# A streaming-encoder trunk on one core: depthwise convolution taps moved from TensorE to ScalarE and GpSimd, three chunks in flight

## The chip, the cores and the metric

The kernel runs on one core of a Trainium2 chip. The metric is device time in microseconds, the median of several executions. A core has TensorE (PE, matrix products into PSUM), VectorE (DVE), ScalarE (ACT), GpSimd (POOL) and SyncE (SP, which here issues the weight loads). PSUM has eight banks; a tile of 128 x 512 float32 fills one.

## The reference

Two layers over 256 tokens of width 2048, in float32. Layer 0 mixes tokens by a Conformer convolution module, layer 1 by latent attention; each is followed by a squared-ReLU MLP. The change touches the convolution module alone:

```python
u = h @ w_pw1 + b_pw1
a, gate = jnp.split(u, 2, axis=-1)
u = a * jax.nn.sigmoid(gate)
u = causal_depthwise_conv(u, w_dw) + b_dw      # 31 taps for each channel
u = jax.nn.silu(layer_norm(u, ln_g, ln_b))
return u @ w_pw2 + b_pw2
```

For each channel the depthwise convolution is a sum of 31 products: the gated row, shifted by w tokens, times one weight for each channel.

## The kernel before, in words

Products of float32 matrices are done as three products of float32r parts: each weight block is split into hi (ScalarE, L154) and lo = raw - hi (L155, on GpSimd in most of the convolution stage).

The 2048 channels are 16 chunks of 128, one channel to a partition, with 256 tokens along the row. The main loop runs c = 1 .. 16; iteration c multiplies chunk c on TensorE (`conv_mm`, L485 to L487, 96 matrix instructions) while the other engines work on chunk c-1. In the order in which they are written, which each engine's queue keeps (the schedule is manual), an iteration holds: weight loads; `glu(c-1)`, where ScalarE takes the sigmoid (L502) and VectorE the gate product (L503) into `ub`, whose 30 leading columns GpSimd clears; the first part of `conv_mm`; weight splits; `pe_taps(c-1)`, which takes the first few taps on TensorE as products with diagonal matrices (L518; ScalarE makes the diagonals, L509) into a PSUM tile `sum`, to which ScalarE adds the bias (L521); `dve_taps`, the remaining taps on VectorE (L552), one SCALAR_TENSOR_TENSOR for each: sum = ub[shifted] * tap + sum; more splits and the rest of `conv_mm`; `to_tokens(c-3)`, which transposes a finished chunk (L579); and GpSimd's addition of the second bias to the residual (L692). Each sum has a tile `sum` of its own, of which it uses half.

Three taps of chunks 1 to 13 go to TensorE, none of chunk 0, six of chunk 14 and 19 of chunk 15. `dve_taps(c)` takes taps of chunk c and of the one before in turn, after four taps of the older chunk alone, and leaves 16 taps of the newest for the next iteration. `ln_stats` puts BATCH_NORM_STATS2 of finished pairs (L589) and a copy of them (L591) between the taps. After the loop come the last transposes, some transposes that keep TensorE busy (`keep_warm`, L220), the LayerNorm (L704, L715, L730 to L737) and the second projection, for which weights are loaded ahead.

The pools of PSUM in this stage are: four tiles `acc` (products, two for each chunk), two `tr` (transposes) and two `sum`.

Of the kernel before, what the change touches and what calls it, by code (L numbers as in the profile page):

```python
# [10 lines left out]
F32 = mybir.dt.float32  # L11
# [3 lines left out]
AF = mybir.ActivationFunctionType  # L15
# [25 lines left out]
PAD_O = 56  # L41
WB = 6
LOOK = WB // 2 - 1
PE_TAPS = (3, 3, 3, 3)
PE_MORE = (3, 16)
LEAD = 4
REST = (16, 12)
N_WARM = 14
N_WARM_LN = (8, 26, 14)
EPS = 1e-6  # L50
# [22 lines left out]
def trunk_kernel(  # L73
# [54 lines left out]
    def nm(s):  # L128
        uid[0] += 1
        return f"{s}_{uid[0]}"  # L130


    def acc_tile():
        return psum["acc"].tile([P, NB], F32, tag="acc", name=nm("acc"))
# [298 lines left out]
    with ExitStack() as cx:  # L433
# [23 lines left out]
        def conv_load(n):  # L457
            if n < NU:
                c, k = n // UC, n % UC * 8
                raws[n] = load(  # L460
                    [rows(conv_w_pw1[0], k, 8, c * P, P), rows(conv_w_pw1[0], k, 8, D + c * P, P)], 8
                )
            elif n < NU + KC // 2:
                raws[n] = load([rows(conv_w_pw2[0], 2 * (n - NU), 2, 0, 2 * NB)], 2)

        def conv_half(n, h):
            if n < NU + KC // 2:
                wjs[n, h] = split_half(raws[n], h, nc.gpsimd if 0 < n + h and n < NU + 2 else nc.vector)
# [10 lines left out]
        def conv_mm(c, k0, nk=4):  # L479
            for k in range(k0, k0 + nk):  # L480
                wh, wl = conv_w(UC * c + k // 8, k % 8)
                for b in range(2):
                    bs = slice(b * P, (b + 1) * P)
                    o = pss[c][b][:, :S]
                    nc.tensor.matmul(o, wh[:, bs], xh(k), start=k == 0, stop=False)  # L485
                    nc.tensor.matmul(o, wh[:, bs], xl(k), start=False, stop=False)  # L486
                    nc.tensor.matmul(o, wl[:, bs], xh(k), start=False, stop=k == KC - 1)  # L487

        pss, ubs, pcs, cas, cts = {}, {}, {}, {}, {}
        n_pe = lambda c: 0 if c == 0 else PE_TAPS[c % 4] + {KC - 2: PE_MORE[0], KC - 1: PE_MORE[1]}.get(c, 0)  # L490
        rest = lambda c: {KC - 2: REST[1], KC - 1: 0}.get(c, REST[0])
        tap = lambda c, w: w_dw[:, w * KC + c : w * KC + c + 1]

        def sum_tile():
            return psum["sum"].tile([P, NB], F32, tag="sum", name=nm("sum"))

        def glu(c):
            ub = ubs[c] = cv2.tile([P, PAD + S], F32, tag="ub", name=nm("ub"), bufs=3)
            nc.gpsimd.memset(ub[:, 0:PAD], 0.0)
            sg = cv2.tile([P, S], F32, tag="sg", name=nm("sg"))  # L500
            va, ga = pss.pop(c)
            nc.scalar.activation(sg, ga[:, :S], AF.Sigmoid, bias=b_pw1[:, KC + c : KC + c + 1])  # L502
            nc.vector.scalar_tensor_tensor(  # L503
                out=ub[:, PAD:], in0=va[:, :S], scalar=b_pw1[:, c : c + 1], in1=sg, op0=ALU.add, op1=ALU.mult
            )

        def diag(c, w):
            dg = cv2.tile([P, P], F32, tag="dg", name=nm("dg"), bufs=16)
            nc.scalar.activation(dg, ident, AF.Copy, scale=tap(c, w))  # L509
            return dg  # L510

        def pe_taps(c, dgs):

            pc = pcs[c] = sum_tile()[:, :S]
            for w in range(n_pe(c)):
                if w == len(dgs):
                    dgs.append(diag(c, w))
                nc.tensor.matmul(pc, dgs[w], ubs[c][:, w : w + S], start=w == 0, stop=w == n_pe(c) - 1)  # L518
            left[c] = list(range(n_pe(c), W))
            if 0 < c < KC - 1:  # L520
                nc.scalar.activation(pc, pc, AF.Identity, bias=b_dw[:, c : c + 1])  # L521
            elif c:

                pcs[c], last_sum[:] = acc_tile()[:, :S], [pc]

        left, last_sum = {}, []

        def ca_part(c):
            if c // 2 not in cas:
                cas[c // 2] = cv2.tile([P, 2, S], F32, tag="ca", name=nm("ca"))  # L530
            return cas[c // 2][:, c % 2, :]

        def dve_tap(c):
            w = left[c].pop(0)
            out = pcs[c]
            if c in (0, KC - 1) and w == n_pe(c):
                nc.vector.tensor_scalar(
                    out, ubs[c][:, w : w + S], scalar1=tap(c, w), scalar2=b_dw[:, c : c + 1],
                    op0=ALU.mult, op1=ALU.add,
                )  # L540
                return
            if c == KC - 1:
                if not left[c]:
                    half = cv2.tile([P, S], F32, tag="half", name=nm("half"), bufs=1)
                    nc.vector.scalar_tensor_tensor(
                        out=half, in0=ubs[c][:, w : w + S], scalar=tap(c, w), in1=out, op0=ALU.mult, op1=ALU.add
                    )
                    nc.vector.tensor_tensor(ca_part(c), last_sum[0], half, op=ALU.add)
                    return
            elif not left[c]:  # L550
                out = ca_part(c)
            nc.vector.scalar_tensor_tensor(  # L552
                out=out, in0=ubs[c][:, w : w + S], scalar=tap(c, w), in1=pcs[c], op0=ALU.mult, op1=ALU.add
            )

        def dve_taps(c, rest, fill):


            n = 0
            while len(left[c]) > rest or left.get(c - 1):  # L560
                if left.get(c - 1):
                    dve_tap(c - 1)
                if n < LEAD and c < KC - 1 and left.get(c - 1):
                    if fill:
                        fill.pop(0)()
                elif len(left[c]) > rest:
                    dve_tap(c)
                n += 1
            while fill:
                fill.pop(0)()  # L570

        def to_tokens(c):

            if c % 2 == 0:
                cts[c // 2] = tr_tile()
            ct = cts[c // 2]
            for t in range(T):
                q = 2 * t + c % 2
                nc.tensor.transpose(  # L579
                    ct[:, q * P : (q + 1) * P], cas[c // 2][:, c % 2, t * P : (t + 1) * P], ident  # L580
                )

        def ln_stats(c):
# [22 lines left out]
        with tc.manual_schedule():  # L606
# [52 lines left out]
                turn(w_dw[:, i * NW : (i + 1) * NW], w_rows[i])  # L659
            conv_split(2)  # L660
            conv_mm(0, 12)
            dgs = []
            fills = []
            for c in range(1, KC + 1):
                n = UC * c
                conv_load(n + 3)
                glu(c - 1)
                fills += ln_stats(c - 4) if c > 3 else []
                fill, fills = fills[: 1 + c % 2], fills[1 + c % 2 :]
                if c < KC:  # L670
                    pss[c] = [acc_tile() for _ in range(2)]
                    conv_mm(c, 0, 2)
                conv_half(n + 1, 0)
                pe_taps(c - 1, dgs)
                conv_half(n + 1, 1)
                dve_taps(c - 1, rest(c - 1), fill)
                conv_load(n + 4)
                if c < KC:
                    conv_mm(c, 2, 6)
                    conv_half(n + 2, 0)  # L680
                    conv_half(n + 2, 1)
                    conv_mm(c, 8)
                    dgs = [diag(c, w) for w in range(min(n_pe(c), 16))]
                if c > 2:
                    to_tokens(c - 3)
                if c < KC:
                    conv_mm(c, 12)
                if 2 <= c < 2 + T * NNB:

                    t, i = divmod(c - 2, NNB)  # L690
                    sl = slice(i * NB, (i + 1) * NB)
                    nc.gpsimd.tensor_tensor(xs[:, t, sl], xs[:, t, sl], b2[:, sl], op=ALU.add)  # L692
            warm(AF.Sqrt)
            keep_warm(ident, N_WARM_LN[0])
            to_tokens(KC - 2)
# [51 lines left out]
            for m in range(NP):  # L747
                if m + 3 < NP:
                    ln_norm(m + 3)
                if m + 2 < NP:  # L750
                    ln_swish(m + 2)
                for j in range(2):
                    k = 2 * m + j
                    wh, wl = conv_w(NU + m, j)
                    for b in range(2):
                        bs = slice(b * NB, (b + 1) * NB)
                        for t in range(T):
                            mm3(ps2[b][t], sh_kt(k, t), sl_kt(k, t), wh[:, bs], wl[:, bs], k == 0, k == KC - 1)
                conv_split(NU + m + 2)
                conv_load(NU + m + 5)  # L760

        ssq, add, prepare = residual_stage(True, g_mlp[0])
        for b in range(2):
# [590 lines left out]
```

## Time and profile before

| what | us |
|---|---|
| median of 3 runs (lowest, highest) | 2014.32 (2014.25, 2014.42) |
| the profiled execution | 2014.3 |
| its span | 2012.4 |
| busy in the span: TensorE | 1989.3 (99%) |
| VectorE | 1217.5 (61%) |
| ScalarE | 966.0 (48%) |
| GpSimd | 209.3 (10%) |
| the chunk loop, first to last gate product (L503) | 31.64 to 222.35 |
| last chunk summed (L548, start and duration) | 232.39, 0.42 |

The profile is of one execution, whose own time lies 1.9 us above its span. A line of the timeline gives the start, the length of a run of like instructions, the engine, the source line, the operation, the tile written and those read, and how many; in brackets stands how long the engine had been idle and who ended that. Instructions of one engine overlap: the start of the next, not the end of this one, tells what one costs. `PE` matrix instructions of float32 come as two records for each product.

### The profile page before, as it was taken

The numbers are of one execution on the slowest core, as the hardware profiler recorded it, in microseconds if no ns is written. First come the engines' busy times: TensorE is split into PE (matmuls) and PEld (weight loads), VectorE is DVE, ScalarE is ACT, GpSimd is POOL, SyncE is SP. The second block draws the span as 40 slices with busy tenths as digits, with TensorE's granted clock in tenths as the row PEclk, the third lists the DMA queues.
The fourth block names the chain that finished last, engine by engine and source line by source line (L and its number), as shares of the span: only waits on it lengthen the run. The fifth ranks groups of instructions, "written<-read, shape, count | busy, mean of one in ns | idle before, by whom it ended". The sixth has DMA issues, their size and how long they took to land.

```text
span 2012.4 us, 28002 instructions
## 1 busy us (share of the span) xinstructions
PE 1989.3 (99%) x11144; PEld 1743.9 (87%) x11144; DVE 1217.5 (61%) x1806; ACT 966.0 (48%) x1372; POOL 209.3 (10%) x156
## 2 busy tenths in 40 slices
PE   7999999999999999999999999999999999999998
PEld 7999888888888888888889998888888888888886
DVE  6999866665554466555546675665654545565453
ACT  5444665544434354444446665544543334454443
POOL 5887300000000000000000510000000000000000
PEclk9999999999999999999999999999999999999999
DMA  7555355666555666555545445666655556665553
GB/s 237 168 168 168 126 188 179 198 189 188 189 197 199 189 189 188 189 192 192 192 144 186 131 146 171 206 190 188 189 192 198 197 188 188 189 189 194 199 192 105
DMA packets 243266, 367.58 MB, mean 183 GB/s; under 512 B 15416, under 2 KB 89792, under 8 KB 242880
## 3 DMA queue, kind: packets, MB, share of 16 engines
q1 hardware_dynamic: 242400, 364.68, 56.9%
q8 instruction: 87, 1.43, 0.3%
q10 hardware_dynamic: 736, 1.12, 0.2%
q14 instruction: 43, 0.35, 0.0%
HBM read 363.68 MB, written 2.10 MB: 182 GB/s over the span
## 4 chain that ended last, share of the span: by engine, by line
PE 96%; DVE 2%; ACT 1%; DMA 0%; issue 0%; POOL 0%; SPq 0%; ACTq 0%; DVEq 0%
PE acc L399 23%; PE acc L182 16%; PE acc L180 16%; PE acc L181 16%; PE acc L400 12%; PE acc L486 3%; PE acc L485 3%; PE acc L487 3%; PE sum L518 1%; PE tr L237 1%; DMA xs<-in_x 0%; PE acc L1128 0%; PE acc L992 0%; PE acc L994 0%; PE acc L993 0%
## 5 line engine op out<-in xcount | busy, mean ns | idle before, releaser
L155 DVE TENSOR_TENSOR lo<-raw,hi 128x1024 fp32r<-128x1024 f32 (+2 forms) x629 | 759.7, 1211 | 694.8 <-ACT hi L154 682.9
L154 ACT ACTIVATE hi<-raw 128x1024 fp32r<-128x1024 f32 (+1 forms) x696 | 723.6, 1046 | 787.3 <-PE acc L181 451.2
L399 PE MATMUL acc<-xt,hi 128*128 128x512 f32 x2048 | 710.6, 390 | 0.0
L400 PE MATMUL acc<-xt,lo 128*128 128x256 f32 x2048 | 577.7, 282 | 0.0
L399 PEld LDWEIGHTS acc<-xt,hi 128*128 128x128 f32 x2048 | 384.4, 188 | 80.5
L180 PE MATMUL acc<-hi,gh 128*128 128x512 f32 x1024 | 398.6, 389 | 0.0
L182 PE MATMUL acc<-lo,gh 128*128 128x512 f32 x1024 | 398.4, 389 | 0.0
L181 PE MATMUL acc<-hi,gl 128*128 128x512 f32 x1024 | 398.4, 389 | 0.0
L400 PEld LDWEIGHTS acc<-xt,lo 128*128 128x128 f32 x2048 | 387.1, 189 | 0.1
L182 PEld LDWEIGHTS acc<-lo,gh 128*128 128x128 f32 x1024 | 192.2, 188 | 39.9
L180 PEld LDWEIGHTS acc<-hi,gh 128*128 128x128 f32 x1024 | 192.2, 188 | 39.8
L181 PEld LDWEIGHTS acc<-hi,gl 128*128 128x128 f32 x1024 | 192.2, 188 | 39.7
L552 DVE SCALAR_TENSOR_TENSOR sum<-ub,w_dw,sum 128x256 f32<-128x256 f32 x404 | 168.5, 483 | 2.8 <-ACT sum L521 0.7
L155 POOL TENSOR_TENSOR lo<-raw,hi 128x1024 fp32r<-128x1024 f32 x67 | 159.3, 2400 | 56.6 <-ACT hi L154 56.6
L485 PE MATMUL acc<-xt,hi 128*128 128x256 f32 x512 | 147.0, 287 | 0.0
L486 PE MATMUL acc<-xt,hi 128*128 128x256 f32 x512 | 143.2, 280 | 1.0 <-DVE xt L193 1.0
L487 PE MATMUL acc<-xt,lo 128*128 128x256 f32 x512 | 143.0, 279 | 0.0
L486 PEld LDWEIGHTS acc<-xt,hi 128*128 128x128 f32 x512 | 96.3, 188 | 1.6 <-DVE xt L193 1.2
L485 PEld LDWEIGHTS acc<-xt,hi 128*128 128x128 f32 x512 | 96.3, 188 | 0.4
L487 PEld LDWEIGHTS acc<-xt,lo 128*128 128x128 f32 x512 | 96.2, 188 | 0.0
L923 POOL MEMSET pad_kv<- 128x8 f32 x1 | 0.1, 105 | 772.6 <-PE acc L182 772.6
L407 ACT ACTIVATE v<-acc 128x256 f32<-128x256 f32 x128 | 46.3, 381 | 25.4 <-PE acc L400 25.4
(230 smaller groups left out, 1787.1 us busy)
## 6 DMA issues: line engine op xcount, KB each, us to landing
raw<-in_mlp_w SPq DMA_DIRECT2D x256, 1024.0 KB, 5.1
raw<-in_conv_w_pw SPq DMA_DIRECT2D x64, 512.0 KB, 5.1
raw<-in_conv_w_pw SPq DMA_DIRECT2D x16, 1024.0 KB, 4.9
raw<-in_mla_w_o SPq DMA_DIRECT2D x16, 1024.0 KB, 5.2
raw<-in_mla_w_kv_up SPq DMA_DIRECT2D x8, 1024.0 KB, 5.4
raw<-in_mla_w_in SPq DMA_DIRECT2D x8, 576.0 KB, 3.7
raw<-in_mla_w_in SPq DMA_DIRECT2D x4, 1024.0 KB, 6.5
raw<-in_mla_w_q_up SPq DMA_DIRECT2D x16, 256.0 KB, 3.6
```

What stands on the lines that cost most here:

```text
L154: nc.scalar.activation(hi, raw[:, js, :], AF.Copy)
L155: eng.tensor_tensor(lo, raw[:, js, :], hi.bitcast(F32), op=ALU.subtract)
L180: nc.tensor.matmul(ps, sh, mh, start=start, stop=False)
L181: nc.tensor.matmul(ps, sl, mh, start=False, stop=False)
L182: nc.tensor.matmul(ps, sh, ml, start=False, stop=stop)
L399: nc.tensor.matmul(ps[b], wh[:, bs], xhl(k), start=k == 0, stop=False)
L400: nc.tensor.matmul(ps[b][:, :S], wl[:, bs], xh(k), start=False, stop=k == KC - 1)
L407: nc.scalar.activation(v[:, b, :], o[:, S:], AF.Copy)
L485: nc.tensor.matmul(o, wh[:, bs], xh(k), start=k == 0, stop=False)
L486: nc.tensor.matmul(o, wh[:, bs], xl(k), start=False, stop=False)
L487: nc.tensor.matmul(o, wl[:, bs], xh(k), start=False, stop=k == KC - 1)
L552: nc.vector.scalar_tensor_tensor(out=out, in0=ubs[c][:, w : w + S], scalar=tap(c, w), in1=pcs[c], op0=ALU.mult, op1=ALU.add)
```

## The change

- The gate product of all chunks but the last goes to GpSimd: ScalarE first copies the value half with its bias from PSUM to SBUF (`vb`), and GpSimd multiplies it by the sigmoid.
- Tap 0 of those chunks is made on ScalarE, together with the bias, and starts the sum in PSUM. Taps 1 and 2 are made by ScalarE as products in SBUF (`product`), which GpSimd adds (`side_sum`); VectorE adds the result to the sum as one of its steps (the entry `None` in `left`, the 15th of 29).
- Only the last chunk has diagonal products: 22 taps, and four more at the side, which leaves VectorE five taps.
- The sums of two neighbouring chunks share one PSUM tile (`pair_part`), two halves of one bank. In the last pair, chunk 14's sum and the product sum of chunk 15 share it; the VectorE part of chunk 15 has an `acc` tile.
- `dve_taps` keeps up to three chunks in flight: it stops when 20 steps are left in all (16 and 18 in the first two iterations), takes in turn from the two oldest chunks, and lets the newest begin after seven steps.
- The first eight blocks of a chunk's product are written in one piece; splits and side sums move in the order; the addition of the second bias on GpSimd moves from the loop to the second projection.

The core of the diff:

```diff
-PE_TAPS = (3, 3, 3, 3)
-PE_MORE = (3, 16)
-LEAD = 4
-REST = (16, 12)
+LAST_PE = 22
+SIDE = 2
+LAST_SIDE = 4
+JOIN = 14
+LEAD = 7
+REST = (16, 18, 20)
...
+        def pair_part(tiles, c, new):
+
+            if c // 2 not in tiles:
+                tiles[c // 2] = new()
+            return tiles[c // 2][:, c % 2 * S : (c % 2 + 1) * S]
...
+                vb = cv2.tile([P, S], F32, tag="vb", name=nm("vb"))
+                nc.scalar.activation(vb, va[:, :S], AF.Identity, bias=b_pw1[:, c : c + 1])
+                nc.gpsimd.tensor_tensor(ub[:, PAD:], vb, sg, op=ALU.mult)
+
+        def product(c, w):
+            pr = cv2.tile([P, S], F32, tag="tp", name=nm("tp"), bufs=LAST_SIDE + SIDE)
+            nc.scalar.activation(pr, ubs[c][:, w : w + S], AF.Copy, scale=tap(c, w))
+            return pr
...
+        def start_sum(c):
+            w = 0
+            if c < KC - 1:
+                pcs_c = pcs[c] = pair_part(sums, c, sum_tile)
+                nc.scalar.activation(
+                    pcs_c, ubs[c][:, 0:S], AF.Identity, bias=b_dw[:, c : c + 1], scale=tap(c, 0)
+                )
+                w = 1
+            else:
+                pcs[c] = acc_tile()[:, :S]
+                o = pair_part(sums, c, sum_tile)
+                last_sum.append(o)
+                for w in range(LAST_PE):
+                    nc.tensor.matmul(o, dgs[w], ubs[c][:, w : w + S], start=w == 0, stop=w == LAST_PE - 1)
+                w = LAST_PE
+            n = LAST_SIDE if c == KC - 1 else SIDE
+            sides[c] = [product(c, w + i) for i in range(n)]
+            left[c] = list(range(w + n, W))
+            left[c].insert(min(JOIN, len(left[c]) - 1), None)
...
+        def side_sum(c):
+            ps = sides[c]
+            step = 1
+            while step < len(ps):
+                for i in range(0, len(ps) - step, 2 * step):
+                    nc.gpsimd.tensor_tensor(ps[i], ps[i], ps[i + step], op=ALU.add)
+                step *= 2
...
+        def dve_taps(c, fill):
+
+
+            n, last = 0, None
+            lead = 0 if c in (0, KC - 1) else LEAD
+            while sum(len(v) for v in left.values()) > rest(c):
+                ready = [k for k in sorted(left) if left[k] and (k < c or n >= lead)]
+                if not ready:
+                    break
+                k = next((k for k in ready[:2] if k != last), None)
+                if fill and (k is None or n % 2 == 1):
+                    fill.pop(0)()
+                    last = None if k is None else last
+                if k is None:
+                    k = ready[0]
+                dve_tap(k)
+                last = k
                 n += 1
...
                 if c < KC:
                     pss[c] = [acc_tile() for _ in range(2)]
-                    conv_mm(c, 0, 2)
-                conv_half(n + 1, 0)
-                pe_taps(c - 1, dgs)
+                    conv_half(n + 1, 0)
+                start_sum(c - 1)
+                if c == KC:
+                    side_sum(c - 1)
+                    conv_half(n + 1, 0)
                 conv_half(n + 1, 1)
-                dve_taps(c - 1, rest(c - 1), fill)
+                dve_taps(c - 1, fill)
                 conv_load(n + 4)
                 if c < KC:
-                    conv_mm(c, 2, 6)
+                    side_sum(c - 1)
+                    conv_mm(c, 0, 8)
```

More of the change, by code (lines that the diff above doesn't have):

```diff
@@ L487, in conv_mm @@
                     nc.tensor.matmul(o, wl[:, bs], xh(k), start=False, stop=k == KC - 1)
-        pss, ubs, pcs, cas, cts = {}, {}, {}, {}, {}
-        n_pe = lambda c: 0 if c == 0 else PE_TAPS[c % 4] + {KC - 2: PE_MORE[0], KC - 1: PE_MORE[1]}.get(c, 0)
-        rest = lambda c: {KC - 2: REST[1], KC - 1: 0}.get(c, REST[0])
+        pss, ubs, pcs, cas, cts, sides, left = {}, {}, {}, {}, {}, {}, {}
+        rest = lambda c: 0 if c == KC - 1 else REST[min(c, 2)]
         tap = lambda c, w: w_dw[:, w * KC + c : w * KC + c + 1]
@@ L495, in sum_tile, with ca_part @@
             return psum["sum"].tile([P, NB], F32, tag="sum", name=nm("sum"))
+        def pair_part(tiles, c, new):
+            if c // 2 not in tiles:
+                tiles[c // 2] = new()
+            return tiles[c // 2][:, c % 2 * S : (c % 2 + 1) * S]
+        def ca_part(c):
+            return pair_part(cas, c, lambda: cv2.tile([P, 2 * S], F32, tag="ca", name=nm("ca")))
         def glu(c):
@@ L502, in glu @@
             nc.scalar.activation(sg, ga[:, :S], AF.Sigmoid, bias=b_pw1[:, KC + c : KC + c + 1])
-            nc.vector.scalar_tensor_tensor(
-                out=ub[:, PAD:], in0=va[:, :S], scalar=b_pw1[:, c : c + 1], in1=sg, op0=ALU.add, op1=ALU.mult
-            )
+            if c == KC - 1:
+                nc.vector.scalar_tensor_tensor(
+                    out=ub[:, PAD:], in0=va[:, :S], scalar=b_pw1[:, c : c + 1], in1=sg, op0=ALU.add, op1=ALU.mult
+                )
[3 more added lines that the diff above has]
+                nc.gpsimd.tensor_tensor(ub[:, PAD:], vb, sg, op=ALU.mult)
@@ L507, in diag @@
+        def product(c, w):
+            pr = cv2.tile([P, S], F32, tag="tp", name=nm("tp"), bufs=LAST_SIDE + SIDE)
+            nc.scalar.activation(pr, ubs[c][:, w : w + S], AF.Copy, scale=tap(c, w))
+            return pr
         def diag(c, w):
-            dg = cv2.tile([P, P], F32, tag="dg", name=nm("dg"), bufs=16)
+            dg = cv2.tile([P, P], F32, tag="dg", name=nm("dg"), bufs=LAST_PE)
             nc.scalar.activation(dg, ident, AF.Copy, scale=tap(c, w))
             return dg
[L512 to L531, printed above, removed]
+        dgs, last_sum = [], []
+        def start_sum(c):
[4 more added lines that the diff above has]
+                    pcs_c, ubs[c][:, 0:S], AF.Identity, bias=b_dw[:, c : c + 1], scale=tap(c, 0)
+                )
+                w = 1
+            else:
+                pcs[c] = acc_tile()[:, :S]
[8 more added lines that the diff above has]
+            left[c].insert(min(JOIN, len(left[c]) - 1), None)
@@ L533, in dve_tap @@
+        sums = {}
+        def side_sum(c):
[5 more added lines that the diff above has]
+                step *= 2
         def dve_tap(c):
@@ L535, in dve_tap @@
             out = pcs[c]
-            if c in (0, KC - 1) and w == n_pe(c):
+            if w is None:
+                nc.vector.tensor_tensor(out, out, sides[c][0], op=ALU.add)
+                return
+            if c == KC - 1 and w == LAST_PE + LAST_SIDE:
                 nc.vector.tensor_scalar(
@@ L541, in dve_tap @@
                 return
-            if c == KC - 1:
-                if not left[c]:
+            if not left[c]:
+                if c == KC - 1:
                     half = cv2.tile([P, S], F32, tag="half", name=nm("half"), bufs=1)
@@ L549, in dve_tap @@
                     return
-            elif not left[c]:
                 out = ca_part(c)
@@ L554, in dve_tap @@
             )
[L556 to L567, printed above, removed]
+        def dve_taps(c, fill):
[13 more added lines that the diff above has]
+                last = k
                 n += 1
@@ L579, in to_tokens @@
                 nc.tensor.transpose(
-                    ct[:, q * P : (q + 1) * P], cas[c // 2][:, c % 2, t * P : (t + 1) * P], ident
+                    ct[:, q * P : (q + 1) * P], ca_part(c)[:, t * P : (t + 1) * P], ident
                 )
@@ L661, in trunk_kernel @@
             conv_mm(0, 12)
-            dgs = []
             fills = []
@@ L682, in trunk_kernel @@
                     conv_mm(c, 8)
-                    dgs = [diag(c, w) for w in range(min(n_pe(c), 16))]
+                    if c > KC - 4:
+                        dgs.extend(diag(KC - 1, w) for w in range(len(dgs), min(len(dgs) + 8, LAST_PE)))
                 if c > 2:
@@ L687, in trunk_kernel @@
                     conv_mm(c, 12)
[L688 to L692, printed above, removed]
             warm(AF.Sqrt)
@@ L760, in trunk_kernel @@
                 conv_load(NU + m + 5)
+                t, i = divmod(m, NNB)
+                sl = slice(i * NB, (i + 1) * NB)
+                nc.gpsimd.tensor_tensor(xs[:, t, sl], xs[:, t, sl], b2[:, sl], op=ALU.add)
         ssq, add, prepare = residual_stage(True, g_mlp[0])
```

## The prediction

> **What bounds the kernel now.** I read the busy table first, then the table by stretches of the conv stage, then the chain of work that ended last, then the timelines of VectorE, ScalarE and TensorE. The whole kernel is TensorE at 99%. For the loop over chunks (43 to 222 us):
>
> ```profile
> 43.00:222.00 179.00, 178.80 (x1454) 176.22 (x1453) 169.07 (x419) 85.25 (x147) 144.04 (x78) 1.00 0.56 166
> ```
>
> The columns are TensorE, its weight loads, VectorE, ScalarE, GpSimd: TensorE has no gap, but VectorE is busy for 169.1 of 179 us, so it can give back 10 us at most. What the diagonal products take stands in the chain:
>
> ```profile
> 68.94 1.31 PE sum L518 x6
> 81.68 1.31 PE sum L518 x6
> ...
> 209.16 2.61 PE sum L518 x12
> ```
>
> Three taps cost 1.31 us, six 2.61. At the end of the loop the chain leaves TensorE and runs through VectorE until the last chunk is summed at 232.81 (232.39 + 0.42).
>
> VectorE's timeline gives two prices for a tap:
>
> ```profile
> 32.81 7.32 DVE L552 SCALAR_TENSOR_TENSOR sum<-ub,w_dw,sum 128x256 f32<-128x256 f32 x14
> ...
> 223.59 0.48 DVE L552 SCALAR_TENSOR_TENSOR sum<-ub,w_dw,sum 128x256 f32<-128x256 f32 x1
> 223.97 0.48 DVE L552 SCALAR_TENSOR_TENSOR acc<-ub,w_dw,acc 128x256 f32<-128x256 f32 x1
> 224.37 0.48 DVE L552 SCALAR_TENSOR_TENSOR sum<-ub,w_dw,sum 128x256 f32<-128x256 f32 x1
> ```
>
> Chunk 0 alone adds 14 times to one sum: (7.32-0.49)/13 = 0.526 us from start to start. Two chunks in turn, each sum in its own bank: 0.392. A tap that follows one it depends on costs 0.134 more.
>
> What counts as dependent is shown elsewhere, on ScalarE:
>
> ```profile
> 21.32 1.65 ACT L186 ACTIVATE xt<-tr,vecs 128x256 fp32r<-128x256 f32 x4
> ...
> 237.49 1.11 ACT L730 ACTIVATE tr<-tr,vecs 128x256 f32<-128x256 f32 x2 [0.89 <-PE tr L725]
> ```
>
> The two L730 work in place on the two halves of one PSUM tile (one bank) and share no element; one lasts 0.537 (its group), so the second starts 1.11-0.54 = 0.57 after the first, when that has ended. The L186, which write SBUF and only read PSUM, start each 0.36 us with 0.56 of duration. So two writers of one PSUM tile run one after the other, even on one engine. Between engines it holds for readers too:
>
> ```profile
> 22.27 1.66 DVE L193 SCALAR_TENSOR_TENSOR xt<-tr,vecs,xt 128x256 fp32r<-128x256 f32 x4 [0.58 <-ACT xt L186]
> ```
>
> This L193 needs only the first half's L186, which ends at 21.88; it starts at 22.27, when the second half's has ended (21.68+0.56 = 22.24).
>
> **The change, part by part.** (1) TensorE loses 13 x 3 + 6 = 45 taps, 13 x 1.31 + 2.61 = 19.6 us. A chunk would then take 12.74 (gating at 68.09, 80.83, 93.57) - 1.31 = 11.43 us. It counts only if VectorE follows.
>
> (2) VectorE loses the gating (0.39 a chunk) and keeps 28 taps (31 less one on ScalarE, two at the side), as now with three on TensorE; it gains a join, which I take at 0.345 (L408, 0.42 busy, overlapped as the taps are; between 0.33 and 0.48). Statistics cost 2 x 0.36 each second chunk. Following the loop by hand, an iteration starts with 7 taps of the older chunks and then takes 22 from the two oldest in turn. The new sums lie two to a bank: chunks 0 and 1, 2 and 3. In an odd iteration the 22 fall on one bank, in an even one on two; there it is the older pair's taps at the start that share.
> Even: 28 x 0.392 + 0.345 + 0.72 + 5 x 0.134 = 12.71. Odd: 28 x 0.392 + 0.345 + 26 x 0.134 = 14.81. For an odd chunk ScalarE's first tap also writes the bank that VectorE is adding to: it comes after iteration before, and VectorE's next tap on that bank after it (0.45, L521); one 0.39 tap covers it but for about 0.1. A pair of chunks: 27.6 us against 25.5 now.
>
> (3) Time line. First gating: ScalarE's sigmoid at 31.13, the new value pass (0.4), GpSimd's product (0.75, row L1050 of the same size), the first tap behind a split; chunk 0 starts on VectorE at 33.4 for 32.2. Chunk 1's first tap is ready at 44.6 (sigmoid 42.33 + 0.4 + 0.4 + 0.75, a split at ScalarE, 0.45). Then iterations 1, 2, 3: 14.16 + 11.48 + 15.17 (27, 7 and 28 dependent taps) to 85.4; five pairs, 138.1, to 223.5; iteration 14 to 236.2. Today chunk 15 is gated at 222.35: 13.9 us later.
>
> (4) Tail. TensorE waits for chunk 15's gating, then runs 22 taps: 0.48 + 0.15 + 44 passes x 0.2155 + 0.16 = 10.3 us. Its sum lies in chunk 14's bank, so VectorE's 18 open steps of chunk 14 wait for it. A gap of TensorE adds a price: the first transposes after the initial wait start each 0.213 us, later ones 0.109; 13 slow ones lost 1.35 us. TensorE, 27.6 - 22.9 = 4.7 us a pair faster than VectorE, will have idled for several us here, so I add 1.35 (bounds 0 and 1.35; no row shows a gap in mid-run). Then 26 steps of VectorE with ten to twelve dependent: 11.7. Last chunk at 236.2 + 10.3 + 1.35 + 11.7 = 259.5 against 232.81: 26.7 later. TensorE idles again before the LayerNorm; slow keep-warm transposes lose 1.35, of which 0.43 is slack today: 0.9.
> On that price the Trainium skill ("TensorE: Matmul & The Clock Gate", Part 1) says that an idle window of about 3.4 us halves the clock until about 3.4 us of work; by it, the two gaps would cost up to 1.7 each, an estimate 1 us above the sum; no mid-run row shows it.
>
> (5) Hidden. GpSimd per chunk: 4 x 2.38 + 2 x 0.75 + 0.13 = 11.2, below 13.8. ScalarE: about 7. DMA: the same 2 MB a chunk, in more time. The b2 adds (8 x 1.30) move to GpSimd's idle time after the loop; they need to be done only at the projection's end. Waits in ScalarE's queue: an odd chunk's first tap holds back the next splits, so TensorE's next 4-block waits about 4 us a pair; its pair needs 22.9 + 1.35 of 27.6, so VectorE is not starved. An even chunk's first tap is ready some 12.2 us after the odd iteration began (first tap 0.5, two products 0.8, split 1.0, GpSimd's split 2.4, a slow 4-block 5.2, then sigmoid, value pass, product and first tap 2.3) and is needed after 14.8 + 3.2 = 18.0: 5.8 us of cover. Beyond it, each microsecond costs 7 (one for each pair).
>
> Sum: 26.7 + 0.9 = 27.6. The profiled execution took 2014.3 (span 2012.4 + 1.9); the median is 2014.32. Forecast **2042 us**; own range 2036 to 2048 (odd wait 0 to 0.5 seven times, joins, clock).
>
> **Rivals.**
> *Order only between engines.* L730 may be ScalarE's own habit; then VectorE's taps in one bank flow at 0.392, but first taps and the 22 products still wait. Iterations are 11.86 and 12.58; chunk 15 is gated at 215.2 (7.2 earlier), the tail of 23.3 stays: 238.5, +5.7 +0.9: **2021**. The Trainium skill ("PSUM — Partial Sum Buffer", PSUM bank collisions raise a hardware error) asks for a guard between two different engines in a bank, which by itself gives this rival; that L193 waited 0.39 us longer than its data agrees, that L730 waited goes beyond it.
> *Halves are independent for all (faster side).* Place: the shared bank; gating at 211.1, 11.2 earlier. The tail still loses: the order puts chunk 15's last addition, which needs the 22 products, ahead of 11 dependent taps of chunk 14 (5.8): 211.1 + 0.48 + 9.8 + 0.42 + 5.8 = 227.6, 5.2 earlier: 2009.1; with both slow clocks **2011**. It decides if odd iterations run at 0.392 and chunk 14 proceeds beside the products. Against it: L730 and L193.
> *The blocked ScalarE queue starves VectorE.* If splits come over 5.8 us late, 7 us for each more: 2 us give 2056. For it: the wait is new. Against it: that slack.
>
> **Chances.** Forecast 0.76, order between engines 0.09, independent 0.10, starved 0.05. The range takes in the second case and goes to 2050; the third and fourth, 0.15, stay out. A measurement tells about 0.2% (4 us) from no change. The third case splits at that line, 0.05 faster and 0.05 same; the first, second and fourth are slower: 0.90.
>
> **What would show it.** Right: taps 0.526 apart in odd iterations, 0.392 in even; iterations of 12.7 and 14.9; gaps on TensorE in the loop; VectorE waiting about 11 us for TensorE's diagonal products, then chunk 14's rest; last chunk near 259. Wrong: taps 0.392 apart throughout, or chunk 14's taps running beside the products; GpSimd's products far above 0.75; or TensorE without gaps.

## The result and the profile after

| | us |
|---|---|
| kernel before, median of 4 runs (lowest, highest) | 2014.28 (2014.05, 2014.42) |
| kernel after, median of 4 runs (lowest, highest) | 2043.18 (2042.66, 2043.50) |
| ratio after / before, 95% interval | 1.0143 (1.0126 to 1.0161) |
| profiled execution after, its span | 2042.66, 2040.9 |

The change makes the kernel 28.9 us slower. The forecast was 2042, with an own range of 2036 to 2048, widened to take in the second case (2021) and to reach 2050.

I read the profile after in the order used for before. First the busy table, and the shares of the chain of work that ended last:

```profile
PE 1986.5 (97%) x11060; PEld 1739.0 (85%) x11060; DVE 1231.2 (60%) x1800; ACT 974.4 (48%) x1380; POOL 231.8 (11%) x189
...
PE 87%; DVE 10%; ACT 1%; issue 1%; DMA 0%; POOL 0%; SPq 0%; ACTq 0%; DVEq 0%
```

TensorE is still the busiest engine by far, but its share fell from 99% to 97%, and a tenth of the chain now runs through VectorE. The table by stretches shows where, in the loop over chunks (TensorE, its weight loads, VectorE, ScalarE, GpSimd, then the granted clock):

```profile
43.00:202.00 159.00, 146.75 (x1176) 143.60 (x1175) 149.52 (x338) 76.21 (x121) 131.57 (x86) 0.96 0.55 160
```

TensorE has 12 us of gaps now; VectorE is busy 149.5 of 159 us. That the missing 9.5 us are no slack of VectorE is seen only in its timeline (start, length, engine, line, operation, count; in brackets what the engine waited for):

```profile
33.38 6.79 DVE L589 SCALAR_TENSOR_TENSOR sum<-ub,w_dw,sum 128x256 f32<-128x256 f32 x13 [4.82 <-ACT sum L542]
...
73.37 12.63 DVE L589 SCALAR_TENSOR_TENSOR sum<-ub,w_dw,sum 128x256 f32<-128x256 f32 x24
...
89.06 10.03 DVE L589 SCALAR_TENSOR_TENSOR sum<-ub,w_dw,sum 128x256 f32<-128x256 f32 x25
...
236.44 0.48 DVE L515 SCALAR_TENSOR_TENSOR ub<-acc,vecs,sg 128x256 f32<-128x256 f32 x1
236.83 0.48 DVE L589 SCALAR_TENSOR_TENSOR sum<-ub,w_dw,sum 128x256 f32<-128x256 f32 x1
248.25 0.49 DVE L589 SCALAR_TENSOR_TENSOR sum<-ub,w_dw,sum 128x256 f32<-128x256 f32 x1 [10.93 <-PE sum L551]
...
253.78 0.43 DVE L586 TENSOR_TENSOR ca<-sum,half 128x256 f32<-128x256 f32 x1
254.24 5.21 DVE L589 SCALAR_TENSOR_TENSOR sum<-ub,w_dw,sum 128x256 f32<-128x256 f32 x10
259.49 0.48 DVE L589 SCALAR_TENSOR_TENSOR ca<-ub,w_dw,sum 128x256 f32<-128x256 f32 x1
```

Three readings. The 24 taps at 73.37 belong to chunks 2 and 3 in turn; the two sums share no element, but they are the halves of one bank, and the taps start (12.63 - 0.49)/23 = 0.528 apart, as if each depended on the one before. One lasts 0.49, so between two of them the profile counts 0.04 as idle, though a tap of the other chunk was there to be done. (Of the 9.5 us, 4.4 are the wait for chunk 1's first tap at 44.57, the only longer one in the loop.) The 25 at 89.06 fall on two banks: (10.03 - 0.49)/24 = 0.398. And at 236.83 VectorE stops for 10.93 us, until the 22 diagonal products of chunk 15 are done, with taps of chunk 14 still to do that need none of them. The last chunk is summed at 259.97 instead of 232.81.

TensorE at the same place:

```profile
237.06 11.14 PE L551 MATMUL sum<-ub,dg 128*128 128x256 f32 x44 [8.11 <-DVE ub L515]
...
260.12 1.08 PE L621 MATMUL tr<-ident,ca 128*128 128x128 f32 x4 [9.64 <-DVE ca L589]
261.00 4.38 PE L222 MATMUL acc<-ident 128*128 128x128 f32 x26
```

It waits 8.1 us for the gating, works 11.1 us, and then waits again, 9.6 us from the end of the keep-warm block behind those products, for the last chunk. The second projection starts at 268.79; before, at 240.42. The 28.4 us between them are nearly the whole difference.

### The profile page after: what moved, and what is told of

Same layout as the page of the kernel before. It is cut to its first block, busy times and chain, and to the rows that moved or that the text cites. A ratio compares the mean times of both kernels' runs of the same rounds, so it can differ in the third digit from the quotient of the medians.

```text
span 2040.9 us, 27871 instructions
## 1 busy us (share of the span) xinstructions
PE 1986.5 (97%) x11060; PEld 1739.0 (85%) x11060; DVE 1231.2 (60%) x1800; ACT 974.4 (48%) x1380; POOL 231.8 (11%) x189
## 4 chain that ended last, share of the span: by engine, by line
PE 87%; DVE 10%; ACT 1%; issue 1%; DMA 0%; POOL 0%; SPq 0%; ACTq 0%; DVEq 0%
PE acc L401 23%; PE acc L184 16%; PE acc L182 16%; PE acc L183 16%; PE acc L402 12%; DVE sum L589 9%; PE tr L239 1%; PE sum L551 1%; PE acc L488 0%; PE acc L487 0%; DMA xs<-in_x 0%; PE acc L489 0%; DVE ca L589 0%; DVE sum L572 0%; PE acc L1172 0%
## 5 line engine op out<-in xcount | busy, mean ns | idle before, releaser
L401 PEld LDWEIGHTS acc<-xt,hi 128*128 128x128 f32 x2048 | 384.4, 188 | 80.4
L589 DVE SCALAR_TENSOR_TENSOR sum<-ub,w_dw,sum 128x256 f32<-128x256 f32 x405 | 182.7, 487 | 28.4 <-PE sum L551 10.9
L489 PE MATMUL acc<-xt,lo 128*128 128x256 f32 x512 | 147.2, 288 | 11.1 <-POOL lo L157 11.1
L487 PEld LDWEIGHTS acc<-xt,hi 128*128 128x128 f32 x512 | 99.8, 195 | 2.8 <-ACT hi L156 2.7
L488 PEld LDWEIGHTS acc<-xt,hi 128*128 128x128 f32 x512 | 99.8, 195 | 0.7 <-DVE xt L195 0.7
```

The source lines that it names most:

```text
L401: nc.tensor.matmul(ps[b], wh[:, bs], xhl(k), start=k == 0, stop=False)
L589: nc.vector.scalar_tensor_tensor(out=out, in0=ubs[c][:, w : w + S], scalar=tap(c, w), in1=pcs[c], op0=ALU.mult, op1=ALU.add)
```

## The experiments

Each run is compared with the kernel before as measured beside it (medians 2014.03 to 2014.43).

My theory: two sums in one bank are one sum as far as the order of work goes. That costs about 2 us in each pair of chunks (dependent spacing in the odd iterations) and holds chunk 14 behind the 22 products in the tail. The rivals: TensorE's gaps, with their slow clock, are the cause; or a queue of ScalarE or GpSimd is. Line numbers of the experiments are their own: in e2, e3 and others a line that is L589 after can be a few lower down.

### e1: a bank of its own for the last chunk's products

```diff
-                o = pair_part(sums, c, sum_tile)
+                o = acc_tile()[:, :S]
```

> The changed kernel, with one edit: the product sum of chunk 15 gets a PSUM tile of its own instead of the second half of chunk 14's. Theory (steps in one PSUM bank run one after the other, between engines and on one engine): VectorE no longer waits 10.9 us for the 22 diagonal products before its second step, it adds chunk 14's taps beside them; but its order puts chunk 15's last addition, which needs the products, ahead of 11 taps of chunk 14, so last chunk at 236.4 + 0.5 + 11.3 + 0.4 + 5.8 = 254.5 instead of 259.97: 5.5 us less than the changed kernel, about 2037.5. The loop before 236 unchanged. Rival (the tail is bound by the products themselves or by VectorE's step count, the bank has no part): no change, 2043.

Measured: 2037.51, ratio to before 1.0115 (1.0102 to 1.0129). The loop is unchanged (chunk 15 gated at 236.43). The shared bank in the tail is worth 5.7 us.

### e2: the same two banks, but neighbours in different ones

```diff
-                pcs_c = pcs[c] = pair_part(sums, c, sum_tile)
+                tid, half = c // 4 * 2 + c % 2, c // 2 % 2
+                if tid not in sums:
+                    sums[tid] = sum_tile()
+                pcs_c = pcs[c] = sums[tid][:, half * S : (half + 1) * S]
```

This is on top of e1. Bank, tile count and instructions stay; only who lies beside whom changes.

> As e1_tail_bank, and the sums are put into the two banks so that neighbouring chunks never share one (chunks 0 and 2, 1 and 3, 4 and 6, ...). Same instructions, same order. Theory: VectorE's taps of two chunks in turn come 0.392 us apart in every iteration, no longer 0.525 in odd ones; two iterations in four wait some 0.6 us for ScalarE's first tap in the bank of the chunk before the last; a pair of chunks 25.0 us instead of 27.6, chunk 15 gated near 218 instead of 236.4, total near 2018 to 2020. Rival (order between engines only, taps of VectorE in one bank were never slowed by the bank but by their own chain or by GpSimd): taps stay 0.525 apart in odd iterations, total as e1_tail_bank, about 2037. Rival (GpSimd or ScalarE sets the pace): total within 3 us of e1_tail_bank.

Measured: 2020.49, ratio 1.0031 (1.0019 to 1.0043). VectorE's timeline of e2, an odd iteration:

```profile
82.75 10.02 DVE L592 SCALAR_TENSOR_TENSOR sum<-ub,w_dw,sum 128x256 f32<-128x256 f32 x25
...
104.96 0.49 DVE L592 SCALAR_TENSOR_TENSOR sum<-ub,w_dw,sum 128x256 f32<-128x256 f32 x1 [1.20 <-ACT sum L545]
```

The same taps on two banks start (10.02 - 0.49)/24 = 0.397 apart. Chunk 15 is gated at 218.93, 17.5 us earlier, and the time falls by 17.0 (the 22 products took 0.6 longer than in e1). This is the largest single cause, and it leaves TensorE's, ScalarE's and GpSimd's work as it was. What remains of the sharing shows in the second line: ScalarE's first tap of a new chunk lands in the bank of an older one. (In e8 below, where it has its own, VectorE's waits for ScalarE's first taps fall from 10.5 us to 5.6 in all, 4.8 of them at the start.)

### e3: the last dependent addition behind chunk 14's rest

On top of e2, in `dve_taps`:

```diff
+                if len(ready) > 1 and ready[1] == KC - 1 and len(left[KC - 1]) == 1:
+                    ready = ready[:1]
```

> As e2_other_bank, and chunk 15's last step waits until chunk 14 is done, so that chunk 14's taps lie beside the 22 products. Theory: tail from gating to the last chunk about 12.3 us instead of 18; total 5 to 6 us below e2_other_bank, about 2012 to 2014, level with the kernel before. Rival (the products, with TensorE's slow clock after its wait, end last anyway): at most 2 us below e2_other_bank.

Measured: 2016.71, ratio 1.0011 (1.0002 to 1.0019): 3.8 us less than e2, where I expected 5 to 6. The tail itself is as expected: gated at 218.85, last chunk at 231.44. What I had not expected comes behind it. VectorE's timeline of e3 in the LayerNorm, steps of two columns:

```profile
233.51 1.34 DVE L204 TENSOR_SCALAR v<-mv 128x2 f32<-128x2 f32 x1
235.11 0.17 DVE L206 RECIPROCAL y<-t 128x2 f32<-128x2 f32 x1 [0.27 <-ACT t L205]
235.31 0.74 DVE L207 TENSOR_TENSOR t<-y 128x2 f32<-128x2 f32 x1
236.09 1.19 DVE L208 TENSOR_TENSOR t<-t,v 128x2 f32<-128x2 f32 x1
```

In the kernel after, the same L204, L207 and L208 take 0.17, 0.16 and 0.16. GpSimd's timeline of e3 at that time:

```profile
227.40 9.86 POOL L809 TENSOR_TENSOR xs<-xs,b 128x512 f32<-128x512 f32 x8
```

These are the moved b2 additions, some 1.23 apart. Each of the three slow steps ends some 0.02 us after one of them does (the records give 234.84, 236.05 and 237.27 for the steps, 234.82, 236.04 and 237.25 for the additions). The RECIPROCAL between them, which has one input, takes its 0.17 although an addition is running (234.76 to 236.04). In the kernel after, the additions were over at 254.8, long before the LayerNorm at 262. An earlier tail has run into work that had been moved to where it was free.

### e4 and e8: a bank for each chunk in flight

```diff
-    repool("c", acc=4, tr=2, sum=2)
+    repool("c", acc=4, tr=1, sum=3)
...
-                pcs_c = pcs[c] = pair_part(sums, c, sum_tile)
+                pcs_c = pcs[c] = sum_tile()[:, :S]
...
-                    pt = acc_tile() if n == 2 else sum_tile() if n == 1 else None
+                    pt = acc_tile() if n == 2 else sum_tile() if n == 1 or j == 1 else None
...
-                turn(w_dw[:, i * NW : (i + 1) * NW], w_rows[i])
+                turn(w_dw[:, i * NW : (i + 1) * NW], w_rows[i], sum_tile())
```

Both also have the edits of e1 and e3, and put the statistics of a pair into one iteration, so that one bank is enough for transposes. The last two edits are e8's alone: they give the transposes ahead of the loop the banks of the sums, which lie idle there.

> As e3_last_late, but each chunk's sum has a bank of its own, three banks in turn, for which the transposes have one bank instead of two (so the statistics and copy of a pair come in one iteration). Theory: no step waits for another chunk's; iterations of 11.9 and 12.6 us, chunk 15 gated near 213, last chunk near 225 to 228, total 2007 to 2010, below the kernel before; the single transpose bank costs a microsecond or so at the start. Rival (TensorE, GpSimd or the weights' loading becomes the bound as VectorE gets faster): gating not before 218, total as e3_last_late or above.

> As e4_three_banks, whose start lost 9.3 us because the first transposes went one at a time through the single transpose bank; here every second of them and the turned tap weights use the banks of the sums, which are free then. Theory: the loop as in e4_three_banks (24.5 us a pair, VectorE's own steps) from chunk 0 on VectorE at 33.4 instead of 42.7, chunk 15 gated near 211, last chunk near 224.5, total 2007 to 2009: below the kernel before by 5 to 7 us. Rival (with 9 us less lead of TensorE, GpSimd or weights fall behind): gating not before 216, total 2012 or more.

Measured: e4 2017.28, ratio 1.0014 (1.0005 to 1.0023), a miss of some 8 us; e8 2008.61, ratio 0.9972 (0.9962 to 0.9983), as expected. In e4 a pair of chunks took 24.47 us, as worked out, but chunk 0 began on VectorE at 42.70 instead of 33.38: the transposes ahead of the loop had one bank and waited for its reader each time. With those two edits chunk 0 begins at 33.10. The table by stretches of e8:

```profile
43.00:202.00 159.00, 157.12 (x1344) 156.51 (x1343) 155.30 (x387) 89.66 (x146) 148.98 (x95) 1.00 0.62 182
```

In the same 159 us in which the kernel after gave VectorE 338 instructions, it now does 387, and TensorE is nearly without gaps again (157.1 of 159 us). The tail of e8, TensorE and then VectorE:

```profile
211.50 12.79 PE L551 MATMUL acc<-ub,dg 128*128 128x256 f32 x44 [7.20 <-DVE ub L515]
```

```profile
224.33 0.42 DVE L586 TENSOR_TENSOR ca<-acc,half 128x256 f32<-128x256 f32 x1 [1.40 <-PE acc L551]
...
228.16 1.07 DVE L204 TENSOR_SCALAR v<-mv 128x2 f32<-128x2 f32 x1
```

Chunk 14 now runs beside the products and VectorE waits only 1.40 us for them. But the products are at their slowest (12.8 us), and the collision with GpSimd is back.

Why they are slowest is seen in the granted clock of TensorE. These are the rows of the table by stretches from the first of the products until the clock changes from 0.50 to 1.00, in the kernel after, in e5 (below) and in e8:

```profile
237.06:239.91 2.85, 2.85 (x7) 2.29 (x8) 0.25 (x1) 2.85 (x6) 1.70 (x3) 0.50 0.02 6
236.90:242.39 5.49, 5.49 (x13) 4.43 (x14) 0.25 (x1) 5.46 (x9) 4.34 (x4) 0.50 0.00 0
211.50:217.69 6.19, 6.19 (x15) 4.93 (x16) 6.12 (x16) 5.03 (x8) 5.11 (x5) 0.50 0.01 3
```

The 44 passes took 11.14, 12.44 and 12.79 us there: the 9.7 that they take at full clock (e6 and e9, below) and half of 2.85, 5.49 and 6.19.

### e5: more work for TensorE in the loop

On top of the kernel after, with the transposes of chunks 0 to 12 done seven times over, with the same result:

```diff
-            for t in range(T):
+            for t in [t for t in range(T) for _ in range(7 if c < KC - 3 else 1)]:
```

> The changed kernel, with each transpose of a finished chunk (chunks 0 to 12) made seven times instead of once: 12 more transposes a chunk at 0.109 us, 1.31 us of TensorE, as much as the three removed taps took; the result is the same. Theory (VectorE sets the pace, TensorE has 4.7 us a pair to spare): no change, 2043 within 2. Rival (TensorE is still the bound of the loop, or its work is in series with VectorE's through the blocked ScalarE queue): 13 x 1.31 = 17 us more, 2060.

Measured: 2044.55 (2043.09 to 2044.97), ratio 1.0149 (1.0134 to 1.0165). From 60 to 210 us TensorE does 1222 products instead of 1095, its granted clock goes from 0.95 to 1.00, and VectorE is busy the same 143.21 us; chunk 15 is gated at 236.28. So neither TensorE's gaps nor its slower clock in the loop cost anything there. Of the 1.4 us more, 1.1 arise in the tail, where VectorE is released by the products at 249.38 instead of 248.25: they ran 5.49 us at the half clock instead of 2.85.

### e6: TensorE kept busy ahead of the 22 products

```diff
+                if c == KC:
+                    keep_warm(ident, 68)
                 start_sum(c - 1)
```

> The changed kernel, with 68 transposes of the identity (7.4 us at 0.109) on TensorE in the gap between chunk 15's product and the 22 diagonal products. Theory (the gap makes TensorE's first products slow): the 44 passes take 9.6 us instead of 11.1, and the end moves by as much: 1.5 us less, 2041.6. Rival (the products are slow for another reason, such as the bank that they share): no change, 2043.

Measured: 2041.34 (2041.09 to 2041.62), ratio 1.0135 (1.0121 to 1.0149), 1.8 us less than after. TensorE's timeline of e6:

```profile
236.94 9.74 PE L551 MATMUL sum<-ub,dg 128*128 128x256 f32 x44 [0.68 <-DVE ub L515]
```

The same 44 passes take 9.74 instead of 11.14: the wait of 8.1 us ahead of them costs 1.4 us.

### e7: the kernel before with shared banks, and nothing else

```diff
-            pc = pcs[c] = sum_tile()[:, :S]
+            if c % 2 == 0:
+                both[:] = [sum_tile()]
+            pc = pcs[c] = both[0][:, c % 2 * S : (c % 2 + 1) * S]
```

> The kernel before, with one part of the change alone: the sums of chunks 2j and 2j+1 lie in one PSUM tile. Theory (one bank, one after the other, on all engines): in an odd chunk VectorE's first step on the older chunk waits for TensorE's three taps and ScalarE's bias (2.3 us), and 22 more taps come 0.525 apart instead of 0.392 (2.95 us); less 1.1 us of waits that VectorE has in a pair, 4.2 us for each of seven pairs, and 8.5 us at the tail where chunk 14 waits for 19 products: about 37 us slower, 2045 to 2055. Rival (order between engines only): 1.2 a pair and the tail, 2031. Rival (no order by bank): 2014.

Measured: 2070.88 (2070.3 to 2072.2), ratio 1.0282 (1.0268 to 1.0296). The sign and the place are as the theory has them, the size is not: 56.7 us slower, where I had 37. VectorE's timeline of e7 over one pair:

```profile
74.38 0.48 DVE L503 SCALAR_TENSOR_TENSOR ub<-acc,vecs,sg 128x256 f32<-128x256 f32 x1 [1.07 <-ACT sg L502]
77.06 13.68 DVE L554 SCALAR_TENSOR_TENSOR sum<-ub,w_dw,sum 128x256 f32<-128x256 f32 x26 [2.20 <-ACT sum L523]
...
107.16 0.48 DVE L503 SCALAR_TENSOR_TENSOR ub<-acc,vecs,sg 128x256 f32<-128x256 f32 x1 [2.25 <-ACT sg L502]
```

A pair takes 32.8 us for 25.5. The 26 taps are (13.68 - 0.49)/25 = 0.528 apart, as expected, and the wait of 2.20 for ScalarE's bias, behind TensorE's taps in the same bank, is there too. I had left out the rest of the circle: TensorE's three taps of the other chunk wait for its late gating (31.8 us in 8 waits), the product of the next chunk stands behind them in TensorE's queue, so the next sigmoid is late, and VectorE waits for that (the 2.25 above). Of the 56.7 us, 46.7 are in the loop (gated at 269.02 for 222.35) and 8.7 in the tail up to the last chunk, as expected there (8.5).

### e9, e10, e11: what is left in e8

e9 is e8 with e6's keep-warm block. e10 is e8 with all gate products back on VectorE:

```diff
-            if c == KC - 1:
+            if True:
```

e11 is e9 with a small GpSimd step ahead of each b2 addition, which reads one column of a late chunk and so holds the addition back until the LayerNorm is over:

```diff
+                k = min(2 * m + 3, KC - 1)
+                nc.gpsimd.tensor_tensor(late, sl_[:, k, 0:1].bitcast(F32), ident[:, 0:1], op=ALU.add)
                 nc.gpsimd.tensor_tensor(xs[:, t, sl], xs[:, t, sl], b2[:, sl], op=ALU.add)
```

> As e8_three_banks_start, with 68 transposes of the identity on TensorE in its gap before the 22 diagonal products, as in e6_warm. Theory: the 44 passes, 12.8 us there after a gap of 7.2 us, take 9.7; VectorE's last addition, which waited 1.4 us for them, follows its own half at once: 1.4 to 2 us less than e8_three_banks_start, about 2007. Rival (VectorE's steps of chunk 14 end last anyway): within 0.5 us of it.

> As e8_three_banks_start, with one part of the change undone: the gating of all chunks is on VectorE again (the value pass on ScalarE and the product on GpSimd go). Theory (VectorE's steps set the pace also with a bank for each sum): 15 times 0.39 us more on VectorE, about 5.9 us slower, 2014 to 2015, so that moving the gating is worth what the whole version gains. Rival (GpSimd, busy 149 of 159 us of the loop, or TensorE sets the pace): not slower than 2010.

> As e9_three_banks_warm, with each addition of the second bias on GpSimd held back until the LayerNorm has made a block that the projection needs (a one-column GpSimd addition that reads it stands ahead), so that none of them runs beside VectorE's small LayerNorm steps. There, in e9_three_banks_warm, the first two-column step lasted 1.16 us for 0.17 and ended 0.03 us after the GpSimd addition that had begun just before it; a second one lasted 0.75 for 0.16. Theory (such a VectorE step with its operands in SBUF waits until the running GpSimd addition has ended): both fall back to 0.17, 1.6 us less, 2006.5. Rival (the steps are slow for another reason, or the additions collide with VectorE's splits in the projection instead): not below 2007.8.

**e9**: 2008.11 (2008.09 to 2009.29), ratio 0.9969 (0.9958 to 0.9981): 0.5 below e8, not the 1.4 to 2 expected and within the spread of the two. The products do take 9.67 us and the last addition starts at 222.98 instead of 224.33, but the LayerNorm, being earlier, meets more of GpSimd's additions:

```profile
226.82 1.16 DVE L204 TENSOR_SCALAR v<-mv 128x2 f32<-128x2 f32 x1
...
228.45 0.74 DVE L207 TENSOR_TENSOR t<-y 128x2 f32<-128x2 f32 x1
```

**e10**: 2013.84 (2013.4 to 2014.68), ratio 0.9998 (0.9989 to 1.0007), level with before and 5.2 above e8, as expected. Fifteen gate products at 0.39 are 5.9 us. With banks of their own for the sums, VectorE's steps set the pace; this part of the change is then worth 5.2 us, nearly the price of its steps.

**e11**: 2009.71 (2008.98 to 2009.82), ratio 0.9978 (0.9969 to 0.9987); the theory said 2006.5, the rival 2007.8 or more. VectorE's timeline of e11:

```profile
226.80 0.17 DVE L204 TENSOR_SCALAR v<-mv 128x2 f32<-128x2 f32 x1
...
227.44 0.16 DVE L207 TENSOR_TENSOR t<-y 128x2 f32<-128x2 f32 x1
...
236.40 3.45 DVE L157 TENSOR_TENSOR lo<-raw,hi 128x1024 fp32r<-128x1024 f32 x2 [0.25 <-ACT hi L156]
```

The small steps are short again, which shows that the additions had held them. The additions now meet VectorE's splits: a pair of splits takes 3.45 instead of 2.36, an addition 2.34 instead of 1.27. But TensorE does not wait for that: it is busy all of 236 to 270 us in e9 and in e11. What cost the lead is TensorE itself. The second projection starts 0.78 us earlier than in e9 (233.36 for 234.14); then its blocks follow each other in 6.03 us instead of 5.91, later in 5.60 instead of 5.44, and by 322 it is 1.19 behind. Its 128x512 passes start 0.233 us apart instead of 0.227, and they still do so from 295 to 299, long after the last addition (over at 272.3). So the number is the rival's, but the collision of additions and splits is not the reason. Why the passes are slower is open; this run has one more tile, `late`, ahead of b2 in its pool, and no run tells whether its place matters.

The best version is e8 or e9, at 2008: 0.3% below the kernel before.

## Why the prediction was right

**Step (1), TensorE's 19.6 us.** Right that they count only if VectorE follows. It does not, and e5 gave TensorE as much work back without slowing the loop.

**Step (2), the shared bank.** Right, and the main term. The spacing in odd iterations was put at 0.526 and is 0.528; a pair of chunks was put at 27.6 and measures 27.6 (four pairs from 99.00 to 209.41, by the last taps of chunks two apart). e2 and e7 show it from both sides. The argument came from another engine's row (ScalarE's L730); *independent halves* and *order only between engines* fall with the odd spacing alone. The latter was what the Trainium skill's rule by itself gives ("PSUM — Partial Sum Buffer", PSUM bank collisions raise a hardware error: guard different engines by bank); here the 0.528 goes beyond it. Whether the chip or the program's own waits make VectorE's taps in one bank wait for each other, no run tells. But the trace shows that the program has such waits: 400 of the 423 taps (L589) carry a wait for a semaphore that only VectorE raises, and the second L730 of each pair carries one for ScalarE's own, while the L186 that start before the one ahead has ended carry none for it. The count that is waited for is not kept in the trace, so the program's waits are the likelier cause, and not a shown one.

**Step (3), the time line.** Chunk 0 at 33.4 (measured 33.38), chunk 1 at 44.6 (44.57), chunk 15 gated at 236.2 (236.44).

**Step (4), the tail.** The 22 products with their start and slow clock were put at 11.65 us from the gating; VectorE is released after 11.81 (236.44 to 248.25). The last chunk was put at 259.5 and is summed at 259.97; of the LayerNorm's delay 0.9 was said, 28.4 - 27.2 = 1.2 measured. The price of the clock in mid-run, the one term without a row, was taken as 1.35 from the first transposes; e6 measures 1.4. That it fits is luck: what is lost is half the time that the products spend at the half clock, 2.85 us here, and the same passes lost 2.7 in e5 and 3.1 in e8, outside the bounds of 0 and 1.35 that I had given. The Trainium skill's rule ("TensorE: Matmul & The Clock Gate", Part 1), up to 1.7, agrees with the 1.4, but not with the 12.79 of e8, which is 3.1 above e9's 9.67 for the same passes.

**Step (5), the hidden parts.** Right for GpSimd's products (0.74, put at 0.75) and for ScalarE's queue: from 45 to 215 us VectorE never waited for it, so the rival of the starved VectorE falls. One detail was off: TensorE's wait for splits is about 2.3 us a pair (0.30 + 2.00), not 4; another 0.59 is for a finished chunk. The b2 additions cost nothing in this kernel, as said, but only because the tail is late: e3, e8 and e9 show their price as soon as it is not.

The sum, 27.6, stands against 28.4 at the second projection and 28.9 in the medians. By the experiments, one after the other, the loss is 17.0 (neighbours in one bank), 5.7 (the products in chunk 14's bank), 3.8 (the order of the last addition), and 2.3 that remain in e3.

## What to carry to other kernels

Before two accumulators are put into the halves of one PSUM bank, look whether they are written in turn: if so, in a kernel with such waits they cost the dependent spacing, and interleaving them gains nothing. With as many banks as chains in flight, and the order of the tail put right, the same change was a small gain. Work that is moved to where it is free stays free only as long as what covers it stays late; look at it again after each improvement.

## What the runs showed of the hardware

- A VectorE tap of 128x256 costs 0.39 to 0.40 us behind one in another bank, and 0.53 behind one in the same bank, whether or not they share elements, in these programs with their waits.
- A GpSimd addition of 128x512 float32 holds VectorE's two-column TENSOR_SCALAR and TENSOR_TENSOR steps until it ends (0.16 to 0.17 became 0.74 to 1.34), but not the RECIPROCAL (0.17). VectorE's splits, which read two SBUF tiles, and such additions hold each other (1.18 became 1.73 each, 1.27 became 2.34). VectorE's taps on two banks, with one input in SBUF and one in PSUM, kept 0.39 to 0.40 while GpSimd was busy 131 of 159 us. The Trainium skill ("SBUF — State Buffer", SBUF: two separate sides) calls the pair of ports that the two engines share an exclusive lock, taken by a VectorE instruction with two SBUF inputs or in a mode that uses both ports; the rows of TENSOR_TENSOR, splits and taps agree. The TENSOR_SCALAR L204 has one input; whether it ran in such a mode, no run here shows.
- What a gap ahead of TensorE's work costs does not follow its length: the same 44 passes took 9.7 us after keep-warm work, 11.1 after a gap of 8.1 us and 12.8 after one of 7.2. In the eight runs with a gap before these 22 products, of 4.6 to 8.1 us, they took 9.7 us and half of the time that the clock was still at 0.50, which was 2.9 to 6.2 us. By the clock's record in the traces a stretch at 0.50 lasted 3.41 us or a multiple of that (6.83 in the kernel after, 10.24 in e5 and e8), so the cost depends on where in such a stretch the work begins.
